# Every other weight slab's second part is subtracted on GpSimd instead of VectorE, and the hold in the inverse is taken out

## The chip, the cores and the metric

The kernel runs on one core of a Trainium2 chip. The metric is the device time of one execution in microseconds (us), as the median of several runs. The engines are TensorE (PE in the profile: matrix products, with PEld for its weight loads), VectorE (DVE), ScalarE (ACT), GpSimd (POOL) and SyncE (SP, which issues most DMAs). Each takes its own queue of instructions in order.

## The reference, cut to what matters

Two blocks follow each other on 256 tokens of width 1024. The first has gated linear attention, a convolutional FFN, attention and a second FFN. The change lies in the second block, which is this (cut):

```
h = _rmsnorm(x, norm_g) * (1 + scale) + shift
p = h @ w_in
c_val, c_gate, c_og, ts, r_og, g_conv, g_rwkv = split(p)
u = causal_depthwise_conv(c_val * sigmoid(c_gate), conv_k)      # 31 taps
y_conv = (silu(layernorm(u)) * silu(c_og)) @ w_conv_out
r, k, v, w_low, a_low = split(token_shift(ts))
state_t = state * w_t - (state @ kk_t) b_t + v_t k_t            # RWKV-7, 16 heads of 64
y_rwkv = (layernorm(o) + bonus) * silu(r_og) @ w_rwkv_out
x = x + gate * ((sigmoid(g_conv) * y_conv + sigmoid(g_rwkv) * y_rwkv) @ w_out)
```

All of it is float32 and has to come out nearly exact.

## The kernel before

**Exact products from two parts.** A weight slab is 128 x 1024 float32 (512 KB). `Weights.load` fetches it by DMA into a `raw` tile (five buffers), ScalarE rounds it to the first part `hi` (L78, type fp32r), and VectorE computes the second part `lo = raw - hi` (L80). `hi` and `lo` have four buffers each. The activations are split in the same way, and `mm3` (L113 to L115) forms a product as hi*hi, lo of the activation*hi, hi*lo. A slab is 24 matmuls of 256 columns. There are 286 loads in the kernel.

**The order of the second block.** `ORDER` lists its steps: `low cvg pr pk pv prep inv gains chain cog gr gc conv cln rout cout wout`. `low` is one slab; `cvg` (the convolution's inputs) 16; `pr`, `pk`, `pv` (r, k, v) 8 each. `prep` forms the decayed factors of the recurrence, in four passes of two 128-row blocks. `inv` inverts the triangular matrices of all chunks and heads: 31 steps of substitution on VectorE, each a product into `sub` and an addition into `X` (the tile LT in the profile), every one of which needs the one before. It ends with transposes of X; then TensorE combines the halves (tiles zp, xp) and `chain` runs the four chunks in sequence. Into `prep`, `inv` and `chain` the code puts slabs of the gates (`fill`, projections srog, scog, gr, gc), so that TensorE has work between dependent steps. The 31 taps of the convolution (L1078, L1080, tile y, 8 channel blocks) run on VectorE; those of blocks 6 and 7 may only start after the inverse.

**What sets the order on an engine.** A planner puts each engine's instructions in a sequence at build time. `issue_after(x)` forces what is written in its block behind x in the queue of the block's engine. `g.w.hold` is such a rule: it is set in `inv` at step 23 to that step's addition, and from then on each `lo` stands behind it on VectorE:

```
with g.tc.issue_after(self.hold.ins) if self.hold else ExitStack():
    nc.vector.tensor_tensor(out=lo[:, :w], in0=raw[:, :w], in1=hi[:, :w].bitcast(F32), op=ALU.subtract)
```

GpSimd does next to nothing: a few memsets, among them those that set X to zero (L851) and to one on its diagonal (L852), and four small copies (L785).

Of the kernel before, what the change touches and what calls it, by code (L numbers as in the profile page):

```python
# [10 lines left out]
F32 = mybir.dt.float32  # L11
F32R = mybir.dt.float32r
AF = mybir.ActivationFunctionType
ALU = mybir.AluOpType
# [32 lines left out]
class Pool:  # L47


    def __init__(self, pool):  # L50
        self.pool = pool
# [8 lines left out]
class Weights:  # L60


    def __init__(self, g):
        self.g = g
        self.n = 0
        self.last = self.hold = None
        self.ready = {}

    def load(self, src, out=None):

        g, nc = self.g, self.g.nc
        w, n = src.shape[-1], self.n
        self.n += 1
        raw = g.wraw.tile([P, 1024], F32, tag="raw", name=f"raw{n}")
        hi, lo = out or [g.wsp.tile([P, 1024], F32R, tag=a, name=f"{a}{n}") for a in ("hi", "lo")]
        with g.tc.issue_after(self.last.ins):
            self.last = nc.sync.dma_start(raw[:, :w], src)
        nc.scalar.copy(hi[:, :w], raw[:, :w])  # L78
        with g.tc.issue_after(self.hold.ins) if self.hold else ExitStack():
            nc.vector.tensor_tensor(out=lo[:, :w], in0=raw[:, :w], in1=hi[:, :w].bitcast(F32), op=ALU.subtract)  # L80
        return hi[:, :w], lo[:, :w]

    def after(self, dst, src):
# [562 lines left out]
def second(g, order):  # L646
    nc, I, cst = g.nc, g.I, g.cst
# [27 lines left out]
    v = Ctx()  # L675
# [167 lines left out]
    def inv():  # L843
        VU = v.VU
        LT = sb.tile([P, 2, 32, 32], F32, name="LT")
        L, X = LT[:, 0], LT[:, 1]
        Lb = VU.rearrange("p (c2 cp) h t -> p cp c2 h t", cp=2)
        for hf in range(2):
            tr = nc.vector.transpose(L[64 * hf:64 * hf + 64], Lb[64:128, hf, :, :, 0:32].rearrange("p c2 h t -> p t c2 h"))
        with g.tc.issue_after(tr.ins):  # L850
            nc.gpsimd.memset(X, 0.0)  # L851
        nc.gpsimd.memset(X.rearrange("p a b -> p (a b)")[:, ::33], 1.0)  # L852
        for s in range(31):
            t = sb.tile([P, 256], F32, tag="e", name=f"sub{s}")
            n, m = 31 - s, s + 1
            tv = t[:, :n * m].rearrange("p (a b) -> p a b", b=m)
            mult(tv, L[:, m:, s:s + 1].to_broadcast([P, n, m]), X[:, s:s + 1, :m].to_broadcast([P, n, m]))
            v.inv = nc.vector.tensor_tensor(out=X[:, m:, :m], in0=X[:, m:, :m], in1=tv, op=ALU.add)
            if s % 4 == 3:
                fill(FI[s // 4])  # L860
            if s == 23:
                g.w.hold = v.inv
        v.TT = sb.tile([P, 2, 16, 64], F32, name="TT")
        with g.tc.issue_after(tr.ins):
            nc.gpsimd.memset(v.TT[:, :, :, 0:32], 0.0)
        X2 = sb.tile([P, 2, 32, 32], F32, name="X2")
        TTm = v.TT.rearrange("p c h t -> p (c h) t")
        for hf in range(2):
            nc.vector.transpose(X2[64:96, hf].rearrange("p m s -> p s m"), X[64 * hf:64 * hf + 32].rearrange("p t s -> p s t"))
        TD = L  # L870
        nc.vector.transpose(TD.rearrange("p m t -> p t m"), X)
        for q in (1, 3, 0, 2):
            p0, dg = 32 * q, q % 2
            nc.scalar.copy(TTm[p0:p0 + 32, :, 32 * dg:32 * dg + 32], TD[p0:p0 + 32])
        zt = X2[:, 0]
        fill(1)
        for b in range(2):
            zp = psum.tile([P, 16, 32], F32, name=f"zp{b}")
            for i in range(16):
                for hf in range(2):  # L880
                    o = 64 * hf + 32
                    nc.tensor.matmul(zp[o:o + 32, i, :], Lb[64:96, hf, b, i, 32:], X2[64:96, hf, 16 * b + i, :], start=True, stop=True)
            for hf in range(2):
                o = 64 * hf + 32
                nc.scalar.copy(zt[o:o + 32, 16 * b:16 * b + 16, :], zp[o:o + 32])
            fill(1)
        for b in range(2):
            xp = psum.tile([P, 16, 32], F32, name=f"xp{b}")
            for i in range(16):
                for hf in range(2):  # L890
                    o = 64 * hf
                    nc.tensor.matmul(xp[o:o + 32, i, :], zt[o + 32:o + 64, 16 * b + i, :], TTm[o + 32:o + 64, 16 * b + i, 32:], start=True, stop=True)
            for hf in range(2):
                o = 64 * hf
                nc.scalar.copy(TTm[o:o + 32, 16 * b:16 * b + 16, 32:], xp[o:o + 32])
            fill(1)
# [127 lines left out]
    def fill(n):  # L1024

        for _ in range(int(n)):
            next(slabs, None)

    def rest(n):
        for _ in gates[n]:  # L1030
            pass
# [92 lines left out]
    def wout():  # L1124
# [3 lines left out]
        def ev(j, ps):  # L1128
            for b in range(2):
                nc.vector.scalar_tensor_tensor(out=g.x[:, j, :], in0=ps[:, b], scalar=g.mod[:, 16 + j:17 + j], in1=g.x[:, j, :], op0=ALU.mult, op1=ALU.add)  # L1130

        project_both(g, I["w_out"], v.mh, ev)

    steps = dict(low=low, pk=pk, pr=pr, pv=pv, prep=prep, inv=inv, chain=chain, gains=gains, cvg=cvg, conv=conv, cln=cln,
                 rout=rout, cout=cout, wout=wout)
    for n in order.split():
        rest(n) if n in gates else steps[n]()


# [154 lines left out]
def body(nc, tc, I, O, stages=("gla", "ffn0", "attn", "ffn1", "second")):  # L1294
    with ExitStack() as es:
# [48 lines left out]
        for s in stages:  # L1344
            if s == "gla":
                gla(g)
            if s == "attn":
                load_const(g, 2)
                attn(g)
            if s == "second":  # L1350
                load_const(g, 3)
                for _ in g.ada:
                    pass
                second(g, ORDER)
                final(g)
            if s.startswith("ffn"):
                if s == "ffn0":
                    load_const(g, 1)
                elif "attn" not in stages:
                    load_const(g, 2)  # L1360
                ffn(g, int(s[3]))
# [14 lines left out]
```

## Time and profile before

| | |
|---|---|
| median of 3 runs | 1015.84 us (1015.53 to 1017.38) |
| profiled execution, its time / its span | 1019.53 / 1017.4 us |
| TensorE busy | 976.7 us (96%) |
| VectorE busy | 829.7 us (82%) |
| ScalarE busy | 613.1 us (60%) |
| GpSimd busy | 5.8 us (1%) |
| subtractions L80, all blocks | 286, 343.7 us busy |

The busy time of an engine is an average over stages with different limits. The span counts from the first to the last instruction; the run's time has a little around it. "Idle before, releaser" says how long an engine stood idle before an instruction and what ended that. [...] The second block begins at about 600 us.

### The profile page before, as it was taken

How to read it: one execution, taken by the hardware profiler on the slowest of the kernel's cores; microseconds unless marked ns; L12 is line 12 of the kernel's file. 1: busy time of each engine (PE TensorE's matmuls, PEld its weight loads, DVE VectorE, ACT ScalarE, POOL GpSimd, SP SyncE). 2: the span in 40 equal slices, each digit the busy share in tenths (PEclk: the TensorE clock that was granted, in tenths of full speed). 3: DMA queues.
4: the chain of work that ended last, by engine and by line, in shares of the span. 5: the costliest groups of instructions: out<-in, count | busy, mean ns of one | idle time of the engine just before them, and what ended most of it. 6: DMA issues, size and time to landing. Idle time of an engine off the chain costs nothing.

```text
span 1017.4 us, 19354 instructions
## 1 busy us (share of the span) xinstructions
PE 976.7 (96%) x7636; PEld 906.7 (89%) x7636; DVE 829.7 (82%) x1529; ACT 613.1 (60%) x1054; POOL 5.8 (1%) x15
## 2 busy tenths in 40 slices
PE   8999999999999999999999999999999969999896
PEld 7988899999888787999999888999988969999895
DVE  5946689888867887999888578999999999857785
ACT  6636667666544577676666457445667617555953
POOL 0000000000000000000000000000000000000000
PEclk8999999999999999999999999999999979999998
DMA  7748256566676851646565675455423334533461
GB/s 266 254 124 274 58 172 190 184 187 196 206 231 223 274 191 42 209 161 207 177 180 168 191 260 196 149 179 184 146 84 103 106 102 158 170 129 126 138 240 42
DMA packets 54442, 175.01 MB, mean 172 GB/s; under 512 B 6320, under 2 KB 12976, under 8 KB 53968
## 3 DMA queue, kind: packets, MB, share of 16 engines
q1 hardware_dynamic: 50464, 169.51, 52.3%
q10 hardware_dynamic: 3888, 4.27, 1.2%
q8 instruction: 60, 0.98, 0.4%
q14 instruction: 30, 0.25, 0.1%
HBM read 168.51 MB, written 5.24 MB: 171 GB/s over the span
## 4 chain that ended last, share of the span: by engine, by line
PE 78%; DVE 12%; ACT 5%; DMA 3%; issue 2%; DVEq 0%; ACTq 0%; SPq 0%
PE up L114 8%; PE up L115 8%; PE up L113 8%; PE dn L120 8%; PE pj L115 7%; PE pj L113 7%; PE pj L114 7%; PE dn L123 4%; PE pj L120 4%; DVE lo L80 3%; PE pt L113 2%; PE pt L114 2%; PE pj L123 2%; PE pt L115 2%; ACT hi L78 1%
## 5 line engine op out<-in xcount | busy, mean ns | idle before, releaser
L78 ACT CAST hi<-raw 128x1024 fp32r<-128x1024 f32 (+2 forms) x286 | 294.9, 1034 | 251.3 <-PE pj L114 95.6
L80 DVE TENSOR_TENSOR lo<-raw,hi 128x1024 fp32r<-128x1024 f32 (+2 forms) x286 | 343.7, 1205 | 84.9 <-ACT hi L78 75.0
L114 PE MATMUL up<-h_f,hi 128*128 128x256 f32 x640 | 181.4, 284 | 0.5 <-DVE h_f L131 0.5
L113 PE MATMUL up<-h_f,hi 128*128 128x256 f32 x640 | 180.8, 283 | 0.3 <-ACT h_f L130 0.3
L115 PE MATMUL up<-h_f,lo 128*128 128x256 f32 x640 | 180.8, 283 | 0.0
L115 PE MATMUL pj<-h_s,lo 128*128 128x256 f32 x544 | 157.7, 291 | 8.9 <-DVE lo L80 8.9
L113 PE MATMUL pj<-h_s,hi 128*128 128x256 f32 x544 | 159.2, 293 | 0.0
L114 PE MATMUL pj<-h_s,hi 128*128 128x256 f32 x544 | 156.5, 288 | 0.0
L120 PE MATMUL dn<-gg,hi 128*128 128x512 f32 x352 | 124.9, 402 | 0.0
L114 PEld LDWEIGHTS up<-h_f,hi 128*128 128x128 f32 x640 | 122.8, 192 | 1.1 <-DVE h_f L131 1.1
L113 PEld LDWEIGHTS up<-h_f,hi 128*128 128x128 f32 x640 | 122.6, 192 | 0.5 <-ACT h_f L130 0.5
L115 PEld LDWEIGHTS up<-h_f,lo 128*128 128x128 f32 x640 | 122.8, 192 | 0.0
L115 PEld LDWEIGHTS pj<-h_s,lo 128*128 128x128 f32 x544 | 106.0, 195 | 10.1 <-DVE lo L80 9.3
L113 PEld LDWEIGHTS pj<-h_s,hi 128*128 128x128 f32 x544 | 105.8, 194 | 1.7
L114 PEld LDWEIGHTS pj<-h_s,hi 128*128 128x128 f32 x544 | 106.0, 195 | 0.7 <-issue 0.3
L123 PE MATMUL dn<-gg,lo 128*128 128x256 f32 x352 | 97.0, 283 | 2.4 <-ACT gg L130 2.4
L1080 DVE SCALAR_TENSOR_TENSOR y<-u,long,y 128x233 f32<-128x233 f32 (+26 forms) x240 | 99.0, 466 | 0.2
L120 PEld LDWEIGHTS dn<-gg,hi 128*128 128x128 f32 x352 | 66.1, 190 | 15.1
L123 PEld LDWEIGHTS dn<-gg,lo 128*128 128x128 f32 x352 | 67.0, 191 | 4.3 <-ACT gg L130 2.9
L257 ACT ACTIVATE y<-up,const 128x256 f32<-128x256 f32 x80 | 44.3, 557 | 1.4 <-DVE y L259 1.2
L259 DVE SCALAR_TENSOR_TENSOR y<-up,const,y 128x255 f32<-128x255 f32 x80 | 38.1, 479 | 1.2
L258 DVE SCALAR_TENSOR_TENSOR y<-up,const,y 128x255 f32<-128x255 f32 x80 | 37.9, 476 | 0.7 <-ACT y L257 0.7
(464 smaller groups left out, 1834.2 us busy)
## 6 DMA issues: line engine op xcount, KB each, us to landing
raw<-w_up SPq DMA_DIRECT2D x88, 512.0 KB, 3.6
raw<-w_down SPq DMA_DIRECT2D x32, 448.0 KB, 3.5
adaw<-ada_w SPq DMA_DIRECT2D x24, 512.0 KB, 4.4
raw<-w_down SPq DMA_DIRECT2D x16, 512.0 KB, 4.4
raw<-w_cvg SPq DMA_DIRECT2D x16, 512.0 KB, 4.2
raw<-gla_v SPq DMA_DIRECT2D x8, 512.0 KB, 5.3
raw<-gla_g SPq DMA_DIRECT2D x8, 512.0 KB, 3.5
raw<-gla_out SPq DMA_DIRECT2D x8, 512.0 KB, 5.3
```

The costliest lines, as they stand in the source:

```text
L78: nc.scalar.copy(hi[:, :w], raw[:, :w])
L80: nc.vector.tensor_tensor(out=lo[:, :w], in0=raw[:, :w], in1=hi[:, :w].bitcast(F32), op=ALU.subtract)
L113: nc.tensor.matmul(ps, lh, rh, start=start, stop=False)
L114: nc.tensor.matmul(ps, lh, rl, start=False, stop=False)
L115: nc.tensor.matmul(ps, ll, rh, start=False, stop=stop)
L120: wide = lambda: nc.tensor.matmul(ps, lhs[0], both, start=first, stop=last)
L123: nc.tensor.matmul(ps[:, 0], lhs[1], both[:, 0], start=False, stop=False)
L257: nc.scalar.activation(yb, ps[:, b, :], AF.Identity, scale=cw[:, 1, c:c + 1], bias=cw[:, 3, c:c + 1])
L258: nc.vector.scalar_tensor_tensor(out=yb[:, 1:], in0=ps[:, b, :T - 1], scalar=cw[:, 0, c:c + 1], in1=yb[:, 1:], op0=ALU.mult, op1=ALU.add)
L259: nc.vector.scalar_tensor_tensor(out=yb[:, :T - 1], in0=ps[:, b, 1:], scalar=cw[:, 2, c:c + 1], in1=yb[:, :T - 1], op0=ALU.mult, op1=ALU.add)
L1080: nc.vector.scalar_tensor_tensor(out=y[:, i:], in0=u[:, :T - i], scalar=w[:, j, 30 - i:31 - i], in1=y[:, i:], op0=ALU.mult, op1=ALU.add)
```

## The change

`Weights` gets a switch `share`. Where it is on, a slab with an odd load number is subtracted by GpSimd (`nc.gpsimd.tensor_tensor`), one with an even number by VectorE as before. `second` sets the switch before each step: off for `low`, `rout`, `cout` and `wout`, on for all others, so from `cvg` up to the convolution branch. Outside the second block it is never on. The hold is taken out: its attribute, its use in `load` and the lines that set it at step 23.

```diff
@@ class Weights
-        self.last = self.hold = None
+        self.last = None
+        self.share = False
@@ load
-        with g.tc.issue_after(self.hold.ins) if self.hold else ExitStack():
-            nc.vector.tensor_tensor(out=lo[:, :w], in0=raw[:, :w], in1=hi[:, :w].bitcast(F32), op=ALU.subtract)
+        eng = nc.gpsimd if self.share and n % 2 else nc.vector
+        eng.tensor_tensor(out=lo[:, :w], in0=raw[:, :w], in1=hi[:, :w].bitcast(F32), op=ALU.subtract)
@@ inv
             if s % 4 == 3:
                 fill(FI[s // 4])
-            if s == 23:
-                g.w.hold = v.inv
@@ second
     for n in order.split():
+        g.w.share = n not in ("low", "rout", "cout", "wout")
         rest(n) if n in gates else steps[n]()
```

The planner makes a new order of it. GpSimd gets 36 subtractions: 2 of slabs that are prefetched before the block's first projection, 28 up to the inverse's last step, 6 after it. From the first projection to the inverse's last step VectorE has 28 in place of 55. The lines behind L63 are shifted by one.

VectorE, in the first third of the inverse, before (`sub` and `LT` are a step's product and addition, `y` a tap, `lo` a slab's second part):

```order
L1080 SCALAR_TENSOR_TENSOR y<-u,long,y 128x241
L650 TENSOR_TENSOR sub_8876<-LT 128x156
L1080 SCALAR_TENSOR_TENSOR y<-u,long,y 128x240
L858 TENSOR_TENSOR LT<-LT,sub_8876 128x26x6
L80 TENSOR_TENSOR lo_9172<-raw_9170,hi_9171 128x1024
L650 TENSOR_TENSOR sub_8879<-LT 128x175
L1080 SCALAR_TENSOR_TENSOR y<-u,long,y 128x239
L858 TENSOR_TENSOR LT<-LT,sub_8879 128x25x7
L1080 SCALAR_TENSOR_TENSOR y<-u,long,y 128x238
L650 TENSOR_TENSOR sub_8882<-LT 128x192
L1080 SCALAR_TENSOR_TENSOR y<-u,long,y 128x237
```

and after, at about the same steps:

```order
L81 TENSOR_TENSOR lo_9080<-raw_9078,hi_9079 128x1024
L651 TENSOR_TENSOR sub_8882<-LT 128x192
L954 SCALAR_TENSOR_TENSOR vf<-vf,long,srog 128x256
L859 TENSOR_TENSOR LT<-LT,sub_8882 128x24x8
L954 SCALAR_TENSOR_TENSOR vf<-vf,long,srog 128x256
L651 TENSOR_TENSOR sub_8952<-LT 128x207
L859 TENSOR_TENSOR LT<-LT,sub_8952 128x23x9
L651 TENSOR_TENSOR sub_8955<-LT 128x220
L859 TENSOR_TENSOR LT<-LT,sub_8955 128x22x10
L651 TENSOR_TENSOR sub_8958<-LT 128x231
L859 TENSOR_TENSOR LT<-LT,sub_8958 128x21x11
```

The 19 taps between the steps are gone; they stand ahead of the preparation now, with all others of the first six channel blocks. Slabs 9046, 9126, 9218, 9341 and 9479 are no longer in VectorE's queue here.

VectorE, behind step 23 of the inverse (`sub_9167`), before:

```order
L650 TENSOR_TENSOR sub_9167<-LT 128x192
L858 TENSOR_TENSOR LT<-LT,sub_9167 128x8x24
L80 TENSOR_TENSOR lo_9218<-raw_9216,hi_9217 128x1024
L650 TENSOR_TENSOR sub_9204<-LT 128x175
L80 TENSOR_TENSOR lo_9272<-raw_9270,hi_9271 128x1024
L858 TENSOR_TENSOR LT<-LT,sub_9204 128x7x25
L80 TENSOR_TENSOR lo_9341<-raw_9339,hi_9340 128x1024
L650 TENSOR_TENSOR sub_9207<-LT 128x156
L80 TENSOR_TENSOR lo_9410<-raw_9408,hi_9409 128x1024
L858 TENSOR_TENSOR LT<-LT,sub_9207 128x6x26
```

and after:

```order
L651 TENSOR_TENSOR sub_9164<-LT 128x207
L81 TENSOR_TENSOR lo_9410<-raw_9408,hi_9409 128x1024
L859 TENSOR_TENSOR LT<-LT,sub_9164 128x9x23
L651 TENSOR_TENSOR sub_9167<-LT 128x192
L859 TENSOR_TENSOR LT<-LT,sub_9167 128x8x24
L651 TENSOR_TENSOR sub_9204<-LT 128x175
L859 TENSOR_TENSOR LT<-LT,sub_9204 128x7x25
L651 TENSOR_TENSOR sub_9207<-LT 128x156
L859 TENSOR_TENSOR LT<-LT,sub_9207 128x6x26
```

The four held subtractions are spread: 9272 and 9410 stand at earlier steps, 9218 and 9341 are GpSimd's. Between the first and the last step there were nine subtractions on VectorE, now there are five.

GpSimd, from the preparation to the inverse, before:

```order
L785 COPY long<-Pp_8277 128x8
L785 COPY long<-Pp_8401 128x8
L785 COPY long<-Pp_8556 128x8
L865 MEMSET TT 128x32x32
L785 COPY long<-Pp_8711 128x8
L851 MEMSET LT 128x1024
L852 MEMSET LT 128x32
```

and after:

```order
L81 TENSOR_TENSOR lo_8639<-raw_8637,hi_8638 128x1024
L786 COPY long<-Pp_8277 128x8
L786 COPY long<-Pp_8401 128x8
L81 TENSOR_TENSOR lo_8794<-raw_8792,hi_8793 128x1024
L786 COPY long<-Pp_8556 128x8
L81 TENSOR_TENSOR lo_8887<-raw_8885,hi_8886 128x1024
L864 MEMSET TT 128x32x32
L786 COPY long<-Pp_8711 128x8
L852 MEMSET LT 128x1024
L81 TENSOR_TENSOR lo_8966<-raw_8964,hi_8965 128x1024
L853 MEMSET LT 128x32
```

The copies and memsets now share GpSimd's queue with the subtractions, and the diagonal's memset (L853) stands behind that of slab 8966.

## Rows read from the trace of the kernel before

**Rows 1.** Busy us (x instructions) of PE, PEld, DVE, ACT, POOL; granted clock; DMA.
```profile
625.00:640.00 15.00, 14.87 (x84) 11.34 (x83) 14.60 (x35) 13.67 (x25) 0.00 (x0) 1.00 0.43 143
640.00:747.00 107.00, 106.93 (x890) 106.16 (x890) 102.89 (x202) 58.41 (x92) 0.00 (x0) 1.00 0.53 169
747.00:798.00 51.00, 46.62 (x494) 42.51 (x493) 49.12 (x90) 35.27 (x66) 4.08 (x7) 1.00 0.24 73
798.00:842.30 44.30, 35.40 (x275) 34.67 (x275) 42.83 (x99) 18.64 (x29) 0.00 (x0) 0.88 0.42 130
...
847.00:930.00 83.00, 82.06 (x1208) 76.60 (x1209) 61.64 (x116) 47.48 (x81) 0.00 (x0) 0.94 0.47 149
```
**Rows 2.** VectorE's two largest groups, 625 to 842.3 us: busy us, mean ns | idle.
```profile
L1080 DVE SCALAR_TENSOR_TENSOR y<-u,long,y 128x255 f32<-128x255 f32 (+26 forms) x180 | 74.3, 460 | 0.0
L80 DVE TENSOR_TENSOR lo<-raw,hi 128x1024 fp32r<-128x1024 f32 x55 | 67.1, 1219 | 3.2 <-ACT hi L78 2.9
```
**Rows 3.** Timeline of VectorE: start us, us, instruction; sixteen taps, then a subtraction.
```profile
633.98 6.34 DVE L1080 SCALAR_TENSOR_TENSOR y<-u,long,y 128x255 f32<-128x255 f32 x16
...
832.47 1.22 DVE L80 TENSOR_TENSOR lo<-raw,hi 128x1024 fp32r<-128x1024 f32 x1
833.60 0.33 DVE L650 TENSOR_TENSOR sub<-LT 128x175 f32<-128x175 f32 x1
```
**Rows 4.** Timeline of VectorE in the inverse: its first step, the middle, the transposes.
```profile
803.51 0.20 DVE L650 TENSOR_TENSOR sub<-LT 128x31 f32<-128x31 f32 x1
...
822.24 0.40 DVE L858 TENSOR_TENSOR LT<-LT,sub 128x247 f32<-128x247 f32 x1
822.56 0.44 DVE L1080 SCALAR_TENSOR_TENSOR y<-u,long,y 128x226 f32<-128x226 f32 x1
822.93 0.40 DVE L650 TENSOR_TENSOR sub<-LT 128x252 f32<-128x252 f32 x1
823.37 0.42 DVE L858 TENSOR_TENSOR LT<-LT,sub 128x252 f32<-128x252 f32 x1
823.82 0.42 DVE L650 TENSOR_TENSOR sub<-LT 128x255 f32<-128x255 f32 x1
...
842.70 4.22 DVE L869 STREAM_TRANSPOSE X<-LT 32x1024 f32<-32x1024 f32 x2
```
**Rows 5.** TensorE's waits, 798 to 862 us: us in total, times, longest.
```profile
PE pj L115 <- DVE lo L80: 8.9, 1, 8.9
```
**Rows 6.** Stretches of 2 us behind that wait, columns as in Rows 1.
```profile
836.00:838.00 2.00, 2.00 (x12) 2.00 (x11) 2.00 (x4) 0.00 (x0) 0.00 (x0) 0.50 0.65 174
...
840.00:842.00 2.00, 2.00 (x19) 2.00 (x18) 1.86 (x6) 1.26 (x2) 0.00 (x0) 1.00 0.89 323
```
**Rows 7.** Timeline of GpSimd in the preparation: copies and memsets.
```profile
748.82 0.34 POOL L785 COPY long<-Pp 128x8 f32<-128x8 f32 x1 [746.61 <-ACT Pp L783]
751.97 0.85 POOL L785 COPY long<-Pp 128x8 f32<-128x8 f32 x1 [2.81 <-ACT Pp L783]
772.08 0.48 POOL L785 COPY long<-Pp 128x8 f32<-128x8 f32 x1 [19.26 <-ACT Pp L783]
785.26 0.95 POOL L865 MEMSET TT<- 128x1024 f32 x1 [12.70 <-PE L L778]
...
790.60 0.16 POOL L852 MEMSET LT<- 128x32 f32 x1
```
**Rows 8.** Timeline of VectorE beside the second and third copy.
```profile
752.08 0.69 DVE L650 TENSOR_TENSOR kb<-qr,Pi 128x512 f32<-128x512 f32 x1
752.68 0.48 DVE L801 SCALAR_TENSOR_TENSOR k<-qr,long,k 128x256 f32<-128x256 f32 x1
...
772.42 0.48 DVE L795 SCALAR_TENSOR_TENSOR qr<-qr,long,rb 128x256 f32<-128x256 f32 x1
```
**Rows 9.** ScalarE: a table load, and the busy time around it (columns as in Rows 1).
```profile
946.50 1.28 ACT L1094 ACT_TABLE_LOAD   x1
...
940.00:960.00 20.00, 17.31 (x133) 16.55 (x133) 14.96 (x36) 19.20 (x33) 0.00 (x0) 0.97 0.42 136
```

## Prediction, before the changed kernel ran

> **What bounds the kernel now.** I read the time by stretches first [rows 1]. The change acts between 625 us, where the second block's projections begin, and 842.3 us, where the inverse ends. In those 217.3 us VectorE is busy 14.60 + 102.89 + 49.12 + 42.83 = 209.4 us, so it idles 7.9 us. TensorE is busy 203.8 us and idles 13.5 us: 0.2 us before 747, 4.4 us in the preparation (747 to 798) and 8.9 us in the inverse (798 to 842.3). Both engines are nearly full, and VectorE is the fuller one. In the preparation and the inverse TensorE is the one that waits. It waits 8.9 us in one piece for a second part [rows 5]. That is the piece that the hold makes: the slabs which the program loads behind step 23 of the inverse may not be subtracted before that step is done, and the first such subtraction starts at 832.47 [rows 3].
>
> Then I read what VectorE does there [rows 2]. Two groups make two thirds of its work: 180 taps of the convolution and 55 subtractions of weight slabs. The taps are nobody's next input; they fill VectorE's gaps. But VectorE takes its queue in order, and the order puts the taps of six channels ahead of the inverse's end. So everything in that queue, wanted soon or not, moves the end of the inverse. Behind it stand the transposes of X [rows 4], and behind these TensorE's zp products, which TensorE takes in order. A microsecond more on VectorE before 842.3 is a microsecond more at the end, as long as VectorE stays the fuller engine.
>
> After 847 VectorE idles 21.4 of 83 us [rows 1], and TensorE sets the pace.
>
> **The change, part by part.**
>
> *Subtractions leave VectorE.* By the order, 36 of them go to GpSimd: 2 before 625 us, 28 before the inverse ends, 6 behind it. One that stood behind the inverse (the hold kept it there) now stands in it, so VectorE has 28 in place of 55. From one subtraction's start to the next instruction's start it is 833.60 - 832.47 = 1.13 us [rows 3]. 27 x 1.13 = **-30.5 us** on VectorE.
>
> *Taps move.* With that room the planner puts all taps of the six channels ahead of the preparation. Nineteen stood between the inverse's steps. There a tap cost little, because it covered the wait of one step for the one before: two steps with a tap between them take 822.93 - 822.24 = 0.69 us, a step alone 823.82 - 823.37 = 0.45 us [rows 4], so the tap cost 0.24 us. In a run of taps one costs (6.34 - 0.46) / 15 = 0.39 us, 0.46 being the length of the last one [rows 2, 3]. 19 x 0.15 = **+2.9 us**.
>
> *GpSimd takes them up.* No row shows a subtraction on GpSimd. I ask two things: how long it holds GpSimd's way to memory, and whether VectorE stands still meanwhile. For the length: GpSimd writes 1024 columns in 0.95 us [rows 7]. A subtraction reads two such streams and writes one. If reads follow each other and the write runs beside them it is 2 x 0.95 = 1.9 us; if all three follow each other, 2.85 us. I take 1.9 plus 0.14, the time that GpSimd's small copies need once they get through (below): 2.04 us, near the lower end because the write can start with the first results.
>
> For the standing still there is one direct sign. GpSimd copies 8 columns four times, and these copies do not take the same time: 0.34, 0.85 and 0.48 us in the three shown [rows 7]. The long one began at 751.97, while VectorE worked on two inputs in SBUF; it ended at 751.97 + 0.85 = 752.82, which is 0.14 us after VectorE left the kb product (752.68) [rows 8]. The third ended at 772.56, again 0.14 us after VectorE's next instruction began (772.42). So GpSimd's reads wait for a VectorE instruction with two SBUF inputs to end. Whether VectorE waits in the same way for GpSimd these rows can't tell: 8 columns are too few to hold anything up, and the instruction at 752.68 took its usual 0.48 us. I take it that the path is one and serves one engine at a time. Taps, slab subtractions and both instructions of an inverse step all read two SBUF tensors.
>
> [...]
>
> 28 x 2.04 = **+57.1 us** on VectorE (53.2 at 1.9, 79.8 at 2.85).
>
> [...]
>
> *Idle time is used up.* A VectorE that is late waits for no one: **-7.9 us**.
>
> *The hold goes.* It makes TensorE's 8.9 us. They don't come off the end by themselves: zp still needs the inverse. TensorE does its slabs earlier and waits at zp. Cost and gain nothing in this forecast.
>
> *Behind the inverse.* Six subtractions, 6 x 2.04 = 12.2 us of GpSimd, beside 21.4 us of VectorE's idle time [rows 1]; hidden, at most 12.2 if the chain's steps meet them. The order also shows one more table load on ScalarE near the convolution branch, where ScalarE is busy 19.20 of 20 us; a load is 1.28 us [rows 9]. It may be hidden; I count it whole, **+1.3 us**.
>
> *GpSimd's queue.* The memsets and small copies now stand among subtractions. The diagonal memset, which the inverse's first step needs, ended at 790.76 [rows 7] and stands behind one more subtraction; that step came at 803.51 [rows 4], 12.7 us later. That covers 2.04 or 2.85 us. A GpSimd library row also appears once, before the first subtraction, with GpSimd idle for hundreds of microseconds. Nothing.
>
> Sum: -30.5 + 2.9 + 57.1 - 7.9 + 1.3 = **+22.9 us**. The profiled span is 1017.4 us (its run 1019.5), the median 1015.84; the difference is put on the median: **1038.7 us**. With 1.9 it is 1034.8, with 2.85 it is 1061.4. A hold of (30.5 - 2.9 + 7.9 - 1.3) / 28 = 1.22 us would change nothing.
>
> **Rivals.**
>
> *GpSimd works beside VectorE (faster).* Then VectorE has 27.6 us less and isn't the bound. TensorE's idle 13.5 us up to 842.3 could go. The inverse allows as much: it starts 4.4 us earlier when the preparation has no waits on TensorE, has 5 subtractions between its steps in place of 9 (4 x 1.13 = 4.5) and 19 taps less (19 x 0.24 = 4.6), in all 13.5. With the table load -12.2: **1003.6 us**. [...] It speaks for this rival that a fill of 1024 columns on GpSimd went at 785 us beside VectorE. Against it: a fill reads nothing, and the copies waited. It decides if a GpSimd subtraction holds VectorE for less than 1.22 us.
>
> *VectorE is kept out for part of the subtraction.* If only one operand's stream gets in its way, the hold is 0.95 us, 28 x 0.95 = 26.6 and the sum -7.6: **1008 us**; between that and 1.9 us lies everything from 1008 to 1035. For it speaks only that nothing shows how long GpSimd keeps the path.
>
> *GpSimd is the one that waits.* VectorE goes on, GpSimd gets the path late, and TensorE waits for second parts from GpSimd. The path's time is the same sum, so it ends at about 1039 too, with other signs (below).
>
> **How the numbers follow.** Kept out for the whole subtraction, by either engine: 0.70, 1035 to 1061. In part: 0.10, half of it slower. Beside each other: 0.20, 1001 to 1006. Forecast 1038.7 us. The range must leave out no more than 0.2: from 1004 to 1061 it leaves out about half of the free case and the tail above 2.85 us. About 0.2%, 2 us, is what a measurement tells from no change. Faster 0.22, same 0.03, slower 0.75.
>
> **What would show it.** Right: VectorE's instructions with two SBUF inputs show some long ones, about 2 us, beside GpSimd's subtractions; starts of taps about 2.4 us apart there; VectorE busy near 100% to the inverse's end, at about 864 us on this trace; TensorE's waits spread over the projections; a wait of zp for X. If GpSimd waits: its subtractions last 3 us and more, and TensorE waits for second parts from GpSimd. Wrong: taps 0.39 us apart beside a running subtraction, TensorE full to 798 us, the inverse ending before 835. The sum falls if GpSimd's subtractions start less than 1.3 us apart when queued, or if VectorE waits for TensorE often before 747.

## The result, and the profile after

The changed kernel took 1064.16 us (median of 4 runs, 1062.65 to 1070.5), the kernel before 1015.68 us beside it: a ratio of 1.0471 (95% interval 1.0443 to 1.0498), slower by some 48 us. The forecast was slower by 22.9 us, 1038.7 us, with a range up to 1061. The direction was right, the size forecast was less than half of the measured one, and the time lies 3 us beyond the range. Where one run of a kernel was slow at a lower clock (hexp_early, 1082.1 us at 0.947, and taps_spread, 1080.8 us at 0.949), the times and ratios given below are those of its other runs.

The profiled execution took 1062.65 us with a span of 1060.8, 43.4 us more than the span before. (The profiled execution of the kernel before was 4 us above that kernel's median, this one is the fastest of its four; so the traces lie nearer to each other than the medians.) These are its stretches, columns as in [rows 1]: the projections from the first product of h (L220) to the first step of the preparation, then the preparation, the inverse up to the transposes of X, and the rest.

```profile
620.19:780.49 160.30, 138.76 (x1024) 131.55 (x1023) 151.55 (x272) 76.88 (x125) 60.62 (x20) 0.95 0.41 132
780.49:832.05 51.56, 46.23 (x491) 42.20 (x491) 38.47 (x67) 34.87 (x66) 13.23 (x11) 1.00 0.23 73
832.05:880.16 48.11, 36.55 (x289) 35.93 (x289) 46.25 (x75) 20.85 (x32) 15.57 (x6) 0.88 0.44 139
880.16:1060.80 180.64, 159.18 (x1743) 149.73 (x1743) 129.13 (x236) 104.29 (x176) 12.19 (x5) 0.92 0.39 131
```

At the same marks the kernel before has:

```profile
618.82:746.72 127.90, 127.70 (x1021) 123.35 (x1020) 123.40 (x251) 76.28 (x124) 0.00 (x0) 1.00 0.51 163
746.72:798.27 51.55, 47.16 (x503) 43.06 (x505) 49.63 (x92) 35.80 (x67) 4.08 (x7) 1.00 0.24 73
798.27:842.70 44.43, 35.53 (x275) 34.80 (x272) 42.96 (x98) 18.77 (x30) 0.00 (x0) 0.88 0.43 132
842.70:1017.40 174.70, 159.48 (x1754) 148.39 (x1753) 129.40 (x243) 104.18 (x178) 0.00 (x0) 0.94 0.42 140
```

So 32.4 of the 43.4 us arose in the projections, none in the preparation, 3.7 in the inverse, 5.9 behind it, and 1.4 ahead of all this. In the preparation VectorE had 11.2 us less to do, and the preparation took as long as before (in a second profile of the same kernel, changed_again, 3.5 us longer).

That GpSimd keeps VectorE out is plain. Two groups of VectorE between 620 and 880 us (busy us, mean ns), which answer to [rows 2]:

```profile
L1079 DVE SCALAR_TENSOR_TENSOR y<-u,long,y 128x254 f32<-128x254 f32 (+24 forms) x180 | 104.4, 633 | 0.5
L81 DVE TENSOR_TENSOR lo<-raw,hi 128x1024 fp32r<-128x1024 f32 x29 | 35.3, 1216 | 11.0 <-ACT hi L79 10.8
```

As many taps as before, 30 us more. The timeline of VectorE shows where, first in the projections, then in the inverse:

```profile
692.12 3.75 DVE L1079 SCALAR_TENSOR_TENSOR y<-u,long,y 128x242 f32<-128x242 f32 x5
696.19 1.98 DVE L1079 SCALAR_TENSOR_TENSOR y<-u,long,y 128x239 f32<-128x239 f32 x5
...
852.37 2.62 DVE L651 TENSOR_TENSOR sub<-LT 128x240 f32<-128x240 f32 x1
855.02 0.41 DVE L859 TENSOR_TENSOR LT<-LT,sub 128x240 f32<-128x240 f32 x1
```

and GpSimd's beside it:

```profile
691.16 2.91 POOL L81 TENSOR_TENSOR lo<-raw,hi 128x1024 fp32r<-128x1024 f32 x1 [2.70 <-ACT hi L79]
...
852.29 2.43 POOL L81 TENSOR_TENSOR lo<-raw,hi 128x1024 fp32r<-128x1024 f32 x1 [3.67 <-ACT hi L79]
```

Five taps beside GpSimd's subtraction of 691.16 take 3.75 us, five without one 1.98: 1.77 us lost. The step of the inverse at 852.37 began 0.08 us after GpSimd's and lasted 2.62 us, not 0.4. GpSimd's own instructions get longer too: its 36 subtractions take between 2.35 and 5.67 us.

```profile
L81 POOL TENSOR_TENSOR lo<-raw,hi x36: 2345/2548/5669, 609.9 to 948.5; 128x1024 fp32r<-128x1024 f32 x36
```

The wait of [rows 5] is gone. In its place, as forecast, TensorE waits at zp for X. From its waits behind 880 us (us in total, times, longest), with a second one that the kernel before doesn't have:

```profile
PE zp L881 <- DVE X L868: 9.3, 1, 9.3
PE pj L114 <- ACT hi L79: 6.7, 2, 6.6
```

No wait of TensorE is put down to a subtraction on GpSimd.

### The profile page after: what moved, and what is told of

It is laid out like the page before. It is cut to its first block, busy times and chain, and to the rows that moved or that the text cites. A ratio compares the mean times of both kernels' runs of the same rounds, so it can differ in the third digit from the quotient of the medians.

```text
span 1060.8 us, 19357 instructions
## 1 busy us (share of the span) xinstructions
PE 986.7 (93%) x7636; PEld 915.2 (86%) x7636; DVE 847.0 (80%) x1493; ACT 614.8 (58%) x1055; POOL 108.1 (10%) x51
## 5 line engine op out<-in xcount | busy, mean ns | idle before, releaser
L81 DVE TENSOR_TENSOR lo<-raw,hi 128x1024 fp32r<-128x1024 f32 (+2 forms) x250 | 300.1, 1203 | 88.6 <-ACT hi L79 81.1
L81 POOL TENSOR_TENSOR lo<-raw,hi 128x1024 fp32r<-128x1024 f32 x36 | 103.2, 2868 | 822.6 <-ACT hi L79 797.6
L115 PE MATMUL up<-h_f,hi 128*128 128x256 f32 x640 | 181.3, 284 | 0.5 <-DVE h_f L132 0.5
L116 PE MATMUL pj<-h_s,lo 128*128 128x256 f32 x544 | 162.6, 299 | 13.3 <-DVE lo L81 13.3
L114 PE MATMUL pj<-h_s,hi 128*128 128x256 f32 x544 | 162.6, 299 | 0.0
L115 PE MATMUL pj<-h_s,hi 128*128 128x256 f32 x544 | 160.7, 295 | 0.0
L1079 DVE SCALAR_TENSOR_TENSOR y<-u,long,y 128x237 f32<-128x237 f32 (+26 forms) x240 | 133.9, 616 | 0.6
L116 PEld LDWEIGHTS pj<-h_s,lo 128*128 128x128 f32 x544 | 109.9, 202 | 16.2 <-DVE lo L81 15.0
L114 PEld LDWEIGHTS pj<-h_s,hi 128*128 128x128 f32 x544 | 109.8, 202 | 1.5
L115 PEld LDWEIGHTS pj<-h_s,hi 128*128 128x128 f32 x544 | 109.9, 202 | 0.6
L121 PEld LDWEIGHTS dn<-gg,hi 128*128 128x128 f32 x352 | 66.5, 192 | 15.2
L614 DVE SCALAR_TENSOR_TENSOR ada<-adaw,long,ada 128x1024 f32<-128x1024 f32 x21 | 26.9, 1280 | 15.2 <-DMA adaw<-ada_w 15.1
```

The costliest lines, as they stand in the source:

```text
L81: eng.tensor_tensor(out=lo[:, :w], in0=raw[:, :w], in1=hi[:, :w].bitcast(F32), op=ALU.subtract)
L114: nc.tensor.matmul(ps, lh, rh, start=start, stop=False)
L115: nc.tensor.matmul(ps, lh, rl, start=False, stop=False)
L116: nc.tensor.matmul(ps, ll, rh, start=False, stop=stop)
L121: wide = lambda: nc.tensor.matmul(ps, lhs[0], both, start=first, stop=last)
L614: nc.vector.scalar_tensor_tensor(out=acc, in0=r, scalar=sc[:, k:k + 1], in1=acc, op0=ALU.mult, op1=ALU.add)
```

## Experiments

Each ratio is to the kernel before on the same chip, in brackets its 95% interval. The stretches of each profile, in us, with the busy time of VectorE and TensorE in the projections (the kernel before and the changed one first; fills_only and hold_and_hexp, which are as hold_only, taps_spread, hexp_early and late_and_hexp are left out). In share_early the first mark comes 5 us sooner than in the changed kernel and the second 2 us later.

| kernel | projections (VectorE, TensorE busy) | preparation | inverse | rest | ratio |
|---|---|---|---|---|---|
| before | 127.9 (123.4, 127.7) | 51.6 | 44.4 | 174.7 | 1 |
| changed | 160.3 (151.6, 138.8) | 51.6 | 48.1 | 180.6 | 1.0471 |
| changed_again | 161.9 (152.8, 139.2) | 55.1 | 47.9 | 182.5 | 1.0500 |
| hold_only | 127.9 (123.2, 127.7) | 51.5 | 51.2 | 164.3 | 0.9974 |
| share_hold | 163.0 (152.8, 138.8) | 57.3 | 46.5 | 181.3 | 1.0464 |
| block_only | 161.8 (156.8, 135.4) | 57.3 | 70.7 | 165.9 | 1.0608 |
| taps_back | 156.9 (131.4, 137.7) | 63.8 | 50.3 | 176.8 | 1.0491 |
| taps_late | 155.9 (139.3, 136.6) | 56.0 | 47.9 | 180.5 | 1.0403 |
| spread_again | 159.8 (147.9, 138.9) | 61.1 | 48.4 | 175.6 | 1.0462 |
| spread_warm | 164.1 (143.3, 152.6) | 60.7 | 47.8 | 183.5 | 1.0518 |
| every_fourth | 139.8 (137.8, 131.0) | 55.6 | 44.6 | 173.4 | 1.0181 |
| share_early | 167.0 (153.1, 143.2) | 49.5 | 43.5 | 172.4 | 1.0304 |
| share_tail | 127.9 (123.3, 127.7) | 51.6 | 53.7 | 169.4 | 1.0053 |

**The price by itself.** Rounds of VectorE instructions beside large GpSimd ones, with none of the kernel's work.

> None of the kernel's work: ten rounds of small instructions on VectorE beside large ones on GpSimd, the output is meaningless. Taps beside GpSimd subtractions (128x1024, two SBUF inputs): if both inputs in SBUF exclude each other, a tap is stretched by the whole of GpSimd's 2.4 us; otherwise 0.39 us throughout. Beside GpSimd fills: 0.39 us, since a fill reads nothing. Beside GpSimd copies (one input): open; shut out too if reading is what counts. [...] VectorE instructions with an input in PSUM: not shut out, if the rule is one of two SBUF inputs; long, if any read of SBUF counts.

VectorE's rounds of 16 taps, beside one fill, three subtractions, six fills and three copies of 128x1024:

```profile
10.01 8.28 DVE L1310 SCALAR_TENSOR_TENSOR y<-u,w,y 128x255 f32<-128x255 f32 x16
...
19.76 14.15 DVE L1310 SCALAR_TENSOR_TENSOR y<-u,w,y 128x255 f32<-128x255 f32 x16
...
35.41 8.28 DVE L1310 SCALAR_TENSOR_TENSOR y<-u,w,y 128x255 f32<-128x255 f32 x16
...
45.17 10.25 DVE L1310 SCALAR_TENSOR_TENSOR y<-u,w,y 128x255 f32<-128x255 f32 x16
```

Each kind of VectorE instruction of all rounds (min/median/max ns); `bank` is in PSUM. All but the taps stood beside GpSimd subtractions only:

```profile
L1310 DVE SCALAR_TENSOR_TENSOR y<-u,w,y x66: 482/484/2444, 5.9 to 116.7; 128x255 f32<-128x255 f32 x66
L1311 DVE TENSOR_SCALAR y<-y,w x16: 407/414/2380, 56.9 to 69.5; 128x256 f32<-128x256 f32 x16
L1312 DVE COPY y<-u x16: 286/294/2382, 71.4 to 82.5; 128x256 f32<-128x256 f32 x16
L1313 DVE SCALAR_TENSOR_TENSOR y<-bank,w,y x16: 478/483/484, 84.3 to 92.1; 128x255 f32<-128x255 f32 x16
L1314 DVE COPY y<-bank x16: 418/424/426, 94.0 to 100.9; 128x256 f32<-128x256 f32 x16
```

Three GpSimd subtractions, beside VectorE instructions with an input in PSUM and then beside VectorE's own subtractions:

```profile
94.33 7.18 POOL L1316 TENSOR_TENSOR gd<-raw,hi 128x1024 f32<-128x1024 f32 x3
104.27 9.89 POOL L1316 TENSOR_TENSOR gd<-raw,hi 128x1024 f32<-128x1024 f32 x3
```

So three take 7.2 us undisturbed, 2.4 each, and cost the taps 14.15 - 8.28 = 5.87 us, 1.96 each. That the rest of the 2.4 runs beside a tap already under way is my reading; it is about the length of one tap (0.48). Fills cost nothing (8.28 us beside six as beside one), copies 1.97 / 3 = 0.66 us each. The taps took 2.44 us at the longest. VectorE's copies and scalar multiply-adds from SBUF are shut out too (2.38 us at the longest), the two kinds with an input in PSUM were not (484 and 426 ns at the longest). The forecast's 2.04 us for a hold came near this, and the first two rivals fall.

**The hold alone, and the sharing alone.** hold_only takes out the hold and leaves every subtraction on VectorE; share_hold keeps the hold for both engines.

```diff
# hold_only, against the changed kernel
-        eng = nc.gpsimd if self.share and n % 2 else nc.vector
-        eng.tensor_tensor(out=lo[:, :w], ...)
+        nc.vector.tensor_tensor(out=lo[:, :w], ...)
# share_hold, against the changed kernel
+        with g.tc.issue_after(self.hold.ins) if self.hold else ExitStack():
             eng.tensor_tensor(out=lo[:, :w], ...)
+            if s == 23:
+                g.w.hold = v.inv
```

> The hold alone goes; all subtractions stay on VectorE. Its order keeps 146 taps ahead of the preparation as before; 7 subtractions more stand between the steps of the inverse. If the loss is GpSimd's reads shutting VectorE out: 1012 to 1026 us, at most 7 x 1.13 = 8 us slower than before in the inverse, some of it given back because TensorE no longer waits 8.9 us there. If a good part of the loss comes from the hold's going: 1035 us or more.

> The sharing alone; the hold of before is kept, for subtractions on GpSimd too. Shut-out theory: 1052 to 1066 us, as the changed kernel, since the projections, where 34 of its 43 us appeared, are untouched by the hold. If the hold's going makes a good part of the loss: 1040 us or less.

hold_only: 1016.53 us, 0.9974 (0.9949 to 0.9999). share_hold: 1067.22 us, 1.0464 (1.0426 to 1.0502). The whole loss is the sharing's. The hold's going moves work from the rest into the inverse (51.2 and 164.3 against 44.4 and 174.7) and gains little: 0.26% in time, with an interval that ends at 0.9999.

**The shutting out without the saving.** GpSimd repeats every second subtraction for nobody, or fills a tile in its place.

```diff
# block_only, cut; every subtraction stays on VectorE, as in hold_only
+        if self.share and n % 2:
+            gd = g.sb.tile([P, 1024], mybir.dt.bfloat16, tag="gdum", bufs=1, name=f"gd{n}")
+            nc.gpsimd.tensor_tensor(out=gd[:, :w], in0=raw[:, :w], in1=hi[:, :w].bitcast(F32), op=ALU.subtract)
# fills_only: a float32 tile, twice nc.gpsimd.memset(gd[:, :w], 0.0)
```

> As hold_only (all subtractions on VectorE, no hold, its order unchanged), and GpSimd repeats every second one into a scratch tile that nobody reads (in bf16, so that it fits). Nothing is saved and no tap is moved, so this shows the price of the shutting out alone. Theory: 28 subtractions up to the inverse's end, each keeping VectorE out for 1.76 (taps in the changed kernel's projections) to 1.96 us (micro), less the 8 us of VectorE's idle time there: 41 to 47 us over hold_only, 1057 to 1068 us. Rival, that the moved order and not the shutting out makes most of the loss: below 1040 us.

> As block_only, but GpSimd fills the scratch tile twice (2 x 0.95 us) in place of each repeated subtraction. If GpSimd's reading shuts VectorE out: as hold_only, 1013 to 1020 us. If any use of GpSimd's way to memory does, or the waiting on its queue: 1035 us or more.

fills_only: 1016.03 us, 0.9971 (0.9950 to 0.9992), as hold_only. But this run doesn't test what it was meant to. The fills wait for nothing, and GpSimd did all 72 of them between 2 and 75 us, long before the second block, as its row of the page shows (40 slices of 25 us):

```profile
POOL 9990000000000000000000000000000000000000
```

That fills cost VectorE nothing rests on the rounds above alone.

block_only: 1080.12 us, 1.0608 (1.0544 to 1.0672), above what was expected: 63.6 us over hold_only, 1.77 for each of 36. On VectorE's own busy time from the projections to the inverse's end it is (281.0 - 223.1) / 32 = 1.81 us for each of the 32 there. So the holds come on the end nearly in full. And the changed kernel, which saves VectorE 36 subtractions on top, 36 x 1.13 = 40.7 us of its queue, is only 1080.12 - 1064.16 = 16 us faster than block_only, or 11 us by its second measurement (changed_again, 1069.54 us, on the same chip as block_only). In the projections the saving is worth 161.8 - 160.3 = 1.5 us, as the planner put taps in the room that it left (below).

**Fewer, earlier, later.** every_fourth shares slabs with `n % 4 == 1`; share_early shares those loaded in `cvg`, `pr`, `pk`, `pv` alone; share_tail those from `chain` on. None has the hold.

> The changed kernel with every fourth slab on GpSimd in place of every second (18 in all, 14 ahead of the inverse's end). If each shared slab costs what it costs in the changed kernel (48 us for 36): about half, 1037 to 1043 us. If the first ones are covered (VectorE has idle time, TensorE the bound for half of the pairs) and the loss grows faster than the count: 1020 to 1035 us. If the waits on queues come whole with the first few: above 1045 us.

> The changed kernel, sharing only the slabs loaded in the projections (20 on GpSimd; none in the inverse, the chain and after). If the 16 later ones cost what share_tail showed (6 of them 6.6 us over hold_only): the projections' 34 us over hold_only's 1016.5 remain, the rest goes, 1043 to 1053 us. If the later ones are hidden, as the prediction said of those behind the inverse: 1060 us or more.

> No hold, and only the slabs loaded from the chain on are shared: 6 subtractions on GpSimd, 4 of them ahead of the inverse's end by their order. Theory: 4 x 1.8 - 4 x 1.1 = 3 us more on VectorE in the inverse, and up to 6 us if the 6 are also what made the changed kernel's tail longer: 1016 to 1026 us. If the tail's 5.9 us come from what went before (clock, slabs late) and not from these: 1014 to 1020 us.

every_fourth: 1036.16 us, 1.0181 (1.0140 to 1.0223); half the subtractions, 38% of the loss, between what the first two theories gave. share_early: 1049.1 us, 1.0304 (1.0257 to 1.0350), as expected if the later ones cost something. share_tail: 1023.12 us, 1.0053 (1.0031 to 1.0075). The late ones are not hidden: 6 of them cost 6.6 us over hold_only, 2.5 in the inverse, into which 3 of them fall, and 5.1 behind it. share_tail alone has both waits that the changed kernel has behind the inverse:

```profile
PE zp L881 <- DVE X L868: 9.7, 1, 9.7
PE pj L114 <- ACT hi L79: 6.7, 2, 6.6
```

and hold_only has them at 3.7 and 3.8 us. Whether VectorE's standing still or GpSimd's lateness makes them longer wasn't tried apart.

**Are taps that the planner drew forward to blame?** With VectorE's room the planner put 186 taps ahead of the preparation, 146 before; 123 of them, not 90, ahead of the first key slab. Three kernels hold them back with `issue_after`: taps_back 40 until the preparation, taps_late the fifth and sixth block until the v projections, taps_spread blocks three to six behind the first r, k and v slab and the first step of the preparation.

```diff
+            if 2 <= j < 6:      # taps_spread; SPREAD = (0, 8, 16, 25): r, k, v, preparation
+                es.enter_context(g.tc.issue_after(g.mixes[SPREAD[j - 2]].ins))
```

> The changed kernel, but the 40 taps that the planner drew forward into the projections may not be issued before the preparation begins, so that 146 stand ahead of it, as before. Theory that the stages don't share VectorE's time (projections full, preparation bound by its own chain): the projections shrink by 40 taps x 0.39 to 0.63 = 16 to 25 us, preparation and inverse grow by less than 8, time 1042 to 1055 us. Rival, that all of VectorE's work up to the inverse's end is one pot, as the prediction summed it: no change beyond the 0.15 us a tap, 1058 to 1068 us.

> The changed kernel, but the taps of the fifth and sixth channel block may not be issued before the v projections begin. The r and k projections, where the trace shows most of the delay arise (from 4.6 us behind at 668 us to 25 at 740), then hold 41 taps in place of 78, the v projections 41 for 25, the preparation 21 for 0. Theory that the delay comes from taps queued ahead of the slabs in these projections: 37 x 0.39 = 14 us come off there, some of it is given back after them (16 taps x 0.39 = 6 us and up to 21 x 0.24 = 5 us): 1050 to 1060 us. Rival, that VectorE's work up to the inverse's end is one pot: unchanged within 5 us, 1060 to 1069 us.

> The changed kernel with its taps held back to where the kernel before has them: the third, fourth, fifth and sixth channel block may start only behind the first slab of the r, k and v projections and the first step of the preparation. 93 taps then stand ahead of the first key slab (90 before, 123 in the changed kernel, 121 in taps_late). Theory: VectorE is overfull only up to there, and the taps drawn forward are paid where it is full and missed where it then idles; 30 taps x 0.39 = 12 us come off the delay at that slab (20 us so far, in every kernel that shares), at least half of it stays to the end: 1051 to 1059 us. Rival, that they cost as much where they go: 1061 to 1068 us.

taps_back: 1069.49 us, 1.0491 (1.0448 to 1.0534); my expectation was wrong and the rival nearer. taps_late: 1059.79 us, 1.0403 (1.0369 to 1.0437), at the seam of the two ranges. By the ratios it is 7 to 10 us faster than the changed kernel: its interval ends below both of that kernel's (1.0443 to 1.0498, and 1.0460 to 1.0540 in changed_again). Its profile doesn't show where: from the first product of h on it takes 440.3 us, against 440.6 in the changed kernel's fastest run and 447.4 in changed_again's. taps_spread: 1067.14 us, 1.0469 (1.0393 to 1.0546), between 1058.7 and 1071.4, in the rival's range. The stretches of taps_back, projections and preparation, show why that kernel gained nothing:

```profile
619.85:776.79 156.94, 137.66 (x1024) 130.66 (x1023) 131.42 (x233) 76.86 (x125) 56.30 (x20) 0.96 0.42 135
776.79:840.62 63.83, 56.84 (x500) 52.07 (x500) 52.04 (x96) 35.55 (x66) 12.30 (x11) 0.81 0.19 59
```

VectorE had 20.1 us less to do in the projections, and these shrank by 3.4. In the rows by 20 us it was full up to 740 us and idle for 23.5 of the 36.8 us left, where TensorE set the pace (busy for 34.5). In the preparation TensorE ran at a mean clock of 0.81, and 500 matmuls took 56.8 us; in the changed kernel 491 took 46.2.

**A wait that looks like a cause.** By the starts of ScalarE's pass over each slab, every kernel that shares in the projections falls back against the kernel before by 6.8 to 7.3 us at one place, the first key slab (spread_warm, below, by 5.4). In the changed kernel's timeline ScalarE waits there for a small load:

```profile
710.57 0.47 ACT L679 ACTIVATE qr<-pj,long 128x256 f32<-128x256 f32 x1
718.51 1.04 ACT L687 CAST hexpk<-hxk 16x1024 fp32r<-16x1024 f32 x1 [7.47 <-DMA hxk<-hexp]
720.26 0.51 ACT L723 ACTIVATE kksq<-qr,long 128x256 f32<-128x256 f32 x1 [0.70 <-DVE qr L680]
```

SyncE issues that load at 714.50 us, behind seven key slabs that it issues from 691.83 on, and its waits there (37.6 us in six, 680 to 722 us) are put down to VectorE's second parts: by the profile, then, it comes late because VectorE is late. hexp_early and late_and_hexp (with taps_late) put it on ScalarE's queue, earlier (cut; the rule that sets its place changes with it):

```diff
-            nc.sync.dma_start(hx, I["hexp"])
+            (nc.scalar if name == "k" else nc.sync).dma_start(hx, I["hexp"])
```

> The changed kernel, but the small load of hexp for the key norms goes through ScalarE's own queue right behind the convolution gates, in place of SyncE's queue behind the slabs of the key projection. In the changed kernel ScalarE waits 7.5 us for it (1.1 us before), the next slab's first part and the key norms stand behind it, and the projections fall back from 15.3 to 22.6 us behind in that one step. Theory that this wait is a term of the loss by itself: 5 to 7.5 us come off, 1056 to 1060 us. Rival, that VectorE, which was 100% busy all through that wait, is the bound there anyway: within 2 us of the changed kernel, 1062 to 1067 us.

> taps_late and hexp_early together. If the two terms are separate: 1059.8 less 5 to 7.5, 1052 to 1055 us. If VectorE sets the projections whatever ScalarE waits for: 1058 to 1062 us.

hexp_early: 1070.78 us, 1.0508 (1.0459 to 1.0557). late_and_hexp: 1068.09 us, 1.0491 (1.0438 to 1.0545). Both lie above both of their ranges. Nothing gained; the step back is still there (7.3 us), and in late_and_hexp ScalarE's timeline names what had stood behind the load all along:

```profile
724.46 0.51 ACT L723 ACTIVATE kksq<-qr,long 128x256 f32<-128x256 f32 x1 [9.30 <-DVE qr L680]
```

VectorE is 9 us behind by then. I read it so: TensorE can run ahead of VectorE by a few buffers, until ScalarE needs the first key slab from VectorE's hand, and there the lead is paid back in one step. (Both profiles also lose 3.8 and 6.5 us more early in the projections. That can't be put down to the change: taps_spread and spread_again, two profiles of the same kernel, differ by 9 us at that place.)

**TensorE's clock.** Stretches of 2 us in the changed kernel around that wait:

```profile
718.00:720.00 2.00, 0.00 (x0) 0.00 (x0) 2.00 (x4) 1.04 (x1) 0.00 (x0) 1.00 0.42 168
720.00:722.00 2.00, 1.18 (x10) 1.18 (x11) 2.00 (x6) 1.74 (x4) 0.00 (x0) 1.00 0.52 147
722.00:724.00 2.00, 2.00 (x12) 2.00 (x11) 2.00 (x3) 1.78 (x4) 1.86 (x1) 0.50 0.28 115
```

TensorE stands still for 2.8 of the first 4 us, and then runs at a granted clock of 0.50, with 12 matmuls in 2 us. Summed over stretches of 1 us up to the inverse's end (busy time times what the clock lacked to 1.00), the lower clock took 2.8 us before, 11.3 in the changed kernel and 20.9 in taps_back. spread_warm fills TensorE's waits in taps_spread with 8 idle matmuls ahead of a shared slab's own; spread_again and changed_again are the kernels to hold it against, on one chip.

```diff
+        if c >= first and getattr(g, "warm", False) and g.w.n % 2 == 0:
+            for _ in range(8):
+                nc.tensor.matmul(ps[:, :T], wh[:, 0, :], h[0][:, 0, :], start=True, stop=True)
```

> taps_spread, and in the projections 8 matmuls more (0.95 us) ahead of each shared slab's own: they need the first part alone, write where the slab's own start overwrites them, and so run while TensorE would wait for GpSimd's or VectorE's second part; some 17 slabs, 16 us of work for TensorE. Theory that the rest of the loss is TensorE at its lower clock after waits (22.9 us lost up to the inverse's end in taps_spread's profile, 11.3 in the changed kernel, 2.8 before): the clock falls less often, 1050 to 1062 us, mean granted clock 0.968 or more. Rival, that the clock only goes with the waiting and costs nothing of its own: 1066 us or more, since TensorE has 16 us more to do, with the clock as in taps_spread.

> taps_spread once more, on the same chip as the two others, since its four times lay between 1058.7 and 1080.8 us and followed the granted clock (0.970 to 0.949). If the clock makes that scatter: again some 1 us for each 0.001 of mean clock, the best runs near 1058 us.

> The changed kernel again, as the measure for the two others: 1062 to 1070 us at a mean clock of 0.964 to 0.970. If taps drawn forward cost nothing at an equal clock, taps_spread's runs lie on the line of time over clock that these make; if they cost, 4 us or more below it.

spread_warm: 1070.7 us, 1.0518 (1.0474 to 1.0562). spread_again: 1065.9 us, 1.0462 (1.0418 to 1.0505), at clocks of 0.954 to 0.968. changed_again: 1069.54 us, 1.0500 (1.0460 to 1.0540), at 0.952 to 0.965. With the idle matmuls the time that the lower clock took, summed in the same way, fell from 20.0 us (spread_again) to 15.2 in the profiles, but the added work cost more than that, and spread_warm lies in the rival's range. So this run doesn't show what the clock costs in the whole kernel. One stretch shows it. The preparation of share_hold has the same matmuls in the same order as that of the changed kernel, and VectorE is busy there for 0.1 us more:

```profile
782.52:839.78 57.26, 51.93 (x491) 47.58 (x491) 38.59 (x66) 34.89 (x66) 11.78 (x11) 0.88 0.21 65
```

At a clock of 0.88 in place of 1.00 TensorE was busy for 5.7 us more (51.93 against 46.23), and the stretch was 5.7 us longer (57.26 against 51.56). And the time of the whole goes with the clock, within one kernel by 0.8 to 0.9 us for each 0.001 of the mean: in the 67 runs of the kernel before (1012.35 us at 0.989, 1024.53 at 0.978) as in those of the changed kernel and of taps_spread. At 0.965 the lines through the ten runs of the changed kernel and the nine of taps_spread stand at 1067.1 and 1062.2 us, and taps_late at 0.967 is 5 to 6 us below the first line. The intervals of the ratios of the changed kernel and taps_spread overlap; so the taps drawn forward cost perhaps 5 us at an equal clock.

**Versions that share nothing.** hold_only, fills_only and hold_and_hexp have no hold and nothing shared.

> hold_only (nothing on GpSimd, no hold) with hexp_early: a version that may be ahead of both kernels. hold_only was 0.26% faster than before; here ScalarE's wait for hexp is 1.1 us, so 0 to 1 us more: 1013 to 1018 us, ratio 0.994 to 0.999.

hold_and_hexp: 1017.31 us, 0.9980 (0.9960 to 1.0000). Without the hold the time is 0.2 to 0.3% lower in all three, at the edge of what the runs can tell from no change (their intervals end at 0.9999, 0.9992 and 1.0000); the load of hexp adds nothing.

## Why the prediction was wrong in size

| term, on this trace | forecast | measured |
|---|---|---|
| VectorE's busy time from the projections to the inverse's end (-30.5 + 2.9 + 57.1) | +29.5 | 236.3 - 216.0 = +20.3 |
| VectorE's idle time there | -7.9 | 23.7 - 7.9 = +15.8 |
| behind the inverse | +1.3 | +5.9 |
| ahead of the projections | 0 | +1.4 |
| sum | +22.9 | +43.4 |

**Right.** The holds were the loss: VectorE's long instructions, the wait of zp for X and the hold's going, which costs nothing, came as written. Of the third rival's two signs one is there, GpSimd's long subtractions, and the other is not: the profile puts no wait of TensorE down to GpSimd. VectorE was not full to the inverse's end, and that came at 880, not 864 us. A hold was sized a little high: by VectorE's own busy time (20.3 + 30.5 - 2.9) / 29 = 1.65 us, 29 being GpSimd's subtractions there, by the other runs 1.77 to 1.96, in place of 2.04. That VectorE stands still for GpSimd at all, on which the +57.1 us rests, no row of the kernel before shows: it was my assumption, and micro and block_only then showed 1.96 and 1.77 us lost for each subtraction. That 2.04 came so near is in part luck: it was meant as the length of a GpSimd subtraction, which is 2.4 us, and VectorE loses less than that length.

**The step that failed is "Idle time is used up".** I put 217 us into one sum, because VectorE idled only 7.9 of them, and took it that an engine that is late waits for no one. That holds where it is the slower of two engines. In the changed kernel it was so in the larger part of the projections, and not behind them: VectorE worked without a break from 660 to 752 us, then it waited again, and up to the inverse's end it idled 15.8 us more than before. Between -7.9 and +15.8 lie 23.7 us, more than the whole miss of 20.5 us. 11.2 of the 15.8 us are in the preparation: 11.2 us less work for VectorE, and the stretch not shorter. The planner had moved the room of the saved subtractions there, by drawing 40 taps forward into the projections. The sum counted those 11.2 us as a gain, and the runs say the same of the whole saving: 30.5 us were forecast for it, and of 40.7 us over all 36 slabs some 11 to 16 reached the end (block_only against the changed kernel). What made VectorE wait is known in part. The delay reaches TensorE as standing still (38.4 us up to the inverse's end, 13.5 before), then as matmuls at a lower clock: 11.3 - 2.8 = 8.5 us more than before up to there, a term that stands in no sum of the forecast. In the preparation such matmuls lengthened the stretch by their whole 5.7 us in share_hold, at a mean clock of 0.88; in the changed kernel's trace the clock stayed at 1.00 there. The planner's order is perhaps 5 us of it at an equal clock, and up to 10 in time (taps_late); the other two ways of moving the taps back changed where VectorE idles, and not clearly the end. How the rest divides between the clock and the two engines waiting for each other by turns stays open, since the run that should have parted them (spread_warm) did not.

**Behind the inverse** I took six subtractions as hidden by 21 us of idle time. share_tail shows 5.1 us there for the three of its six that come late, with the same two waits as the changed kernel. Idle time of an engine is no cover when the steps that are late are the ones that the next engine waits for. The added table load is real (31 on ScalarE, 30 before) and was not tried alone.

**The bounds.** The range ended at 1061 because its upper end was the longest hold, 2.85 us, in the same single sum. A sum by stretches, each with its own slower engine and no gain where VectorE wasn't that, gives for the projections, with the hold as measured since, 127.9 us plus 20 holds of 1.8 less the 4.5 us that VectorE idled there, 159.4 us (160.3 measured), if the room of the saved subtractions goes to taps; and nothing back in the preparation. The rows of the kernel before had the sign: up to 747 us TensorE idled 0.2 us and VectorE 4.5, so there the fuller engine was TensorE.

## What to carry to other kernels

Work moved to a second engine can cost the first one most of the length of the second's instruction: here a GpSimd subtraction of 2.4 us cost VectorE 1.8 us, for 1.13 us saved, for each slab. Sum gains and losses stretch by stretch: a microsecond taken from an engine counts only where that engine is the slower one, while here the microseconds lost reached the end nearly in full. Look in the trace whether a test did its work where it was meant to: fills_only told nothing, since its 72 fills ran half a millisecond too early. And a wait that the profile names may cover another behind it: take it away before calling it a cause.

## What the runs showed that was not expected

- A plain copy and a scalar multiply-add of VectorE with one SBUF input were shut out nearly as long as taps (2.38 us at the longest, taps 2.44, beside 2.4 us subtractions), and a multiply-add with PSUM and SBUF inputs was not (484 ns at the longest).
- GpSimd loses time too: three of its subtractions beside VectorE's own (128x1024) took 9.89 us, 7.2 undisturbed; in the changed kernel one took 5.67.
- After TensorE had stood still, the granted clock was at 0.50 for 3 to 14 us at a time up to the inverse's end (3.4 to 6.8 us in the changed kernel, 13.7 at the longest in taps_back), and one kernel's runs spread by 15 us along the mean clock (spread_again, 1058.2 us at 0.968 to 1073.5 at 0.954).
